# Two-layer trunk in three-pass fp32: the residual enters PSUM through ScalarE, GpSimd sums weights by an accumulating DMA, and seven of eight row pairs use seven products

## The chip, the cores and the metric

One Trainium2 chip, one core, one launch. The metric is the device time of the whole program in microseconds (us). The kernel before has a median of 2328.24 us over 3 runs (2327.93 to 2328.25).

## The reference

A decoder trunk of two layers on 256 tokens of width 2048, with 256 memory tokens. Each layer is a mixer (an HGRN2 recurrence in layer 0, gated linear attention in layer 1) beside a cross-attention into the memory, an output projection, and a SwiGLU feed-forward network (FFN) of inner width 5632. The change is in the FFN, for the greater part:

```python
D_MODEL = 2048; SEQ = 256; D_FF = 5632
hn = _rmsnorm(h, norm_ffn[layer])
gate, up = jnp.split(hn @ w_gate_up[layer], 2, axis=-1)
h = h + (jax.nn.silu(gate) * up) @ w_down[layer]
```

All operands are float32.

## The kernel before, in words

**Three passes.** TensorE (PE) multiplies in a rounded 32-bit format. Every operand is therefore kept as a rounded high part and the remainder, its low part, and every product is three matmuls: high by high, high by low, low by high. For weights, `split` (L201) makes the two parts of a slice of the raw tile: ScalarE (ACT) writes the high part with a cast (L207), VectorE (DVE) subtracts it from the raw slice (L208). The pair of parts lies in one of six buffers of the pool "parts". The raw weights come by DMAs that SyncE (SP) issues, into one of four "raw" buffers. One raw buffer holds four slices of 512 columns, 1 MB.

**Up projection of a block.** The FFN (`ffn`, L820) goes through the 5632 inner columns in 11 blocks of 512, for each of two layers. `up_block` calls `project_halves` (L321): the 16 row blocks of 128 of the gate and the up matrix are taken as 8 row pairs, and for each pair the 2 by 2 block product (two row blocks, gate and up columns; two token tiles) is added to seven PSUM banks, p1 to p7. `KINDS` gives the kind of each pair. A pair of kind S takes seven products (a Strassen-like form), 21 matmuls of 128x128 by 128x512; kinds O and H take eight products, 24 matmuls. Blocks 3 to 10 use the last entry of `KINDS`, "SSOSSOSS" before. `Forms` (L284 to L318) makes the left-hand factors of each pair, once in a layer; `PAIRS` sets what they hold.

For an S pair the four raw slices are split in two parts, a (one slice, L344) and b (two slices, L345), then overwritten by four sums of themselves: DVE makes them in L350 (1024 elements to the partition), L351 and L352 (512 each). The sums are split as parts c and d (two slices each, L353 and L354). Parts are named by the number of the raw tile: the second FFN's block 6, from which the prediction quotes, has pairs 352 to 359, so 353c is part c of its second pair. An O pair has two parts of two slices and no sums.

**Epilogue of a block.** ACT copies bank p1 into e0 (L828), DVE adds the other six banks in seven operations (L831), ACT takes silu (L833), DVE multiplies (L834). The result s is transposed and split into a "quad" (L148 on ACT, L149 on DVE) by a piece that `later` queues and `step` calls at fixed points of the PE program.

**Down projection.** After a block's up projection come two `down` calls: each projects a part of the blocks (two quads from the second part on; `PARTS`) on 512 of the 2048 output columns. `project` (L220) loads 1 MB of weights for each quad, splits it as two parts (names parts_0 and parts_2) and runs 24 matmuls on each of two token tiles' banks, named fd. Then `add_h` (L411) adds the two banks to h in SBUF, with a DVE operation each (L414). The last part of a layer's FFN (`end`) is followed by the next norm's work.

**What sets the order.** Nothing is scheduled by hand in the FFN: a tile framework takes the code in its order, gives buffers from pools and lets its scheduler place each engine's instructions. Each engine runs its list in that order. So where an instruction stands in its engine's list, and which buffer it has to wait for, decide together. Parts are made ahead of PE as far as the six buffers let them. PSUM has eight banks; a block's up projection takes seven.

Of the kernel before, what the change touches and what calls it, by code (L numbers as in the profile page):

```python
# [35 lines left out]
def trunk_kernel(ctx: ExitStack, tc: tile.TileContext, x, mem, norm_mix, norm_ffn, norm_mem,  # L36
# [164 lines left out]
    def split(src, name, by=2):  # L201
# [3 lines left out]
        for k in range(0, n, by):  # L205
            j = min(k + by, n)
            nc.scalar.copy(out=both[:, 0, k:j, 0:m], in_=src[:, k:j, :])  # L207
# [12 lines left out]
    def project(quads, order, w, c0, n, name, parts=None, prep=None, by_tile=None):  # L220
# [5 lines left out]
        ps = [[mm_ps(f"{name}_{i}_{t}") for t in range(NT)] for i in range(len(parts))]  # L226
        if by_tile is None:
            groups = [([qi], range(NT)) for qi in range(len(order))]
        else:
            groups = [(range(len(order)), [t]) for t in range(NT)]  # L230
        got = {}
        for qis, ts in groups:
            for qi in qis:
# [5 lines left out]
                for k, (hi, lo) in enumerate(got[qi]):  # L239
                    if k == 2 or (k == 0 and qi > 0):  # L240
                        step()
                    first = qi == 0 and k == 0
                    last = qi == len(order) - 1 and k == 3
                    for t in ts:
                        xh = quads[q].h[:, k, t * P:(t + 1) * P]
                        xl = quads[q].l[:, k, t * P:(t + 1) * P]
                        for i, (o, m) in enumerate(parts):
                            acc = ps[i][t][:, 0:m]
                            nc.tensor.matmul(acc, xh, hi[:, o:o + m], start=first, stop=False)  # L249
                            nc.tensor.matmul(acc, xh, lo[:, o:o + m], start=False, stop=False)  # L250
                            nc.tensor.matmul(acc, xl, hi[:, o:o + m], start=False, stop=last)  # L251
# [15 lines left out]
    PAIRS = "SSOSSOSB"  # L267
# [4 lines left out]
    class Forms:  # L272
# [20 lines left out]
        def put(self, ps, gains):  # L293
# [15 lines left out]
            nc.vector.scalar_tensor_tensor(out=g[:, 4, :], in0=g[:, 0, :], scalar=-1.0, in1=g[:, 3, :],  # L309
                                           op0=ALU.mult, op1=ALU.subtract)  # L310
            tt(out=g[:, 5, :], in0=g[:, 1, :], in1=g[:, 0, :], op=ALU.subtract)
            tt(out=g[:, 6, :], in0=g[:, 3, :], in1=g[:, 5, :], op=ALU.subtract)
            tt(out=g[:, 7, :], in0=g[:, 2, :], in1=g[:, 6, :], op=ALU.subtract)
# [7 lines left out]
    def project_halves(forms, kinds, w, c0, c1, name):  # L321
# [15 lines left out]
        for p, kind in enumerate(kinds):  # L337
# [7 lines left out]
            if kind == "S":  # L345
                tt = nc.vector.tensor_tensor
                b00, = split(raw[:, 0:1, :], f"{i}a")
                b11, b10 = split(raw[:, 2:4, :], f"{i}b")

                tt(out=raw[:, 0:2, :], in0=raw[:, 0:4:2, :], in1=raw[:, 1:2, :].broadcast_to([P, 2, 512]), op=ALU.subtract)  # L350
                tt(out=raw[:, 2, :], in0=raw[:, 2, :], in1=raw[:, 0, :], op=ALU.add)  # L351
# [468 lines left out]
    def ffn(l, forms, r, after, tail=None):  # L820
# [21 lines left out]
        def down(i, n):  # L842
# [7 lines left out]
            if end:  # L850
                after(n)
# [104 lines left out]
```

## Time and profile before

| what | value |
|---|---|
| median of 3 runs (range) | 2328.24 us (2327.93 to 2328.25) |
| the profiled execution's own time | 2328.0 us |
| its span, first to last instruction | 2326.2 us (1.8 us lie outside) |
| granted PE clock | 0.999 of full speed |
| data moved | 435.51 MB, 187 GB/s mean |
| matmuls and transposes on PE | 11034 |
| block 0, 1, 2 of the second FFN | 44.5, 52.6, 57.4 us |
| blocks 3 to 10, each | 63.2 us (block 6 of the first FFN, 732.50 to 795.60, 63.1 us) |

The profile is one execution. Its rows give a start in us from the start of the span, a duration, the engine, the source line, the operation, output and inputs, shape and type, and, in square brackets, how long the engine had been idle before and what released it. A duration runs from start to end; two neighbours on DVE or ACT overlap by a little, so that the distance of their starts is the better price. The starts of neighbouring matmuls are closer than their durations, since PE is pipelined. Line numbers are those of the kernel before unless the text says after; line 208 of before is 218 of after, 207 is 217, 828 is 842, 831 is 845, 833 is 847, 834 is 848.

### The profile page before, as it was taken

What the parts mean: (1) busy time and instruction counts of PE and PEld (TensorE: products, weight loads), DVE (VectorE), ACT (ScalarE), POOL (GpSimd) and SP (SyncE); (2) the same over time, 40 slices, a digit from 0 to 9 for tenths busy, and PEclk for the clock granted to TensorE, in tenths of its full rate; (3) what the DMA queues carried; (4) which work ended last, traced back from release to release, by engine and by line L of the source; (5) the groups of instructions that cost most, each with busy time, mean ns of one, the idle gap of its engine ahead of it and who ended that gap; (6) DMA issues with size and microseconds to landing.
All of it is one profiled execution on the core that took longest, in us unless ns stands there. A gap on an engine that the chain in (4) does not pass through costs nothing.

```text
span 2326.2 us, 28901 instructions
## 1 busy us (share of the span) xinstructions
PE 2303.5 (99%) x11034; PEld 1940.7 (83%) x11034; DVE 1888.0 (81%) x2262; ACT 1261.2 (54%) x1643; POOL 22.2 (1%) x39
## 2 busy tenths in 40 slices
PE   9999999999999999999999999999999999999998
PEld 7888888888887888888889999988887888888886
DVE  5565565668999999999985664557999999999995
ACT  7543535356555655555555654356555555555563
POOL 0000000000000000000000000000000000000000
PEclk9999999999999999999999999999999999999999
DMA  8554445454556555556565445455465656656563
GB/s 315 193 172 159 163 145 181 136 190 164 198 181 214 196 188 202 196 202 209 187 226 166 150 147 167 152 198 174 166 214 189 208 183 209 205 186 213 200 217 127
DMA packets 229211, 435.51 MB, mean 187 GB/s; under 512 B 10028, under 2 KB 38992, under 8 KB 228816
## 3 DMA queue, kind: packets, MB, share of 16 engines
q1 hardware_dynamic: 227776, 429.40, 54.8%
q10 hardware_dynamic: 1296, 4.26, 0.5%
q8 instruction: 86, 1.41, 0.2%
q14 instruction: 53, 0.43, 0.1%
HBM read 430.48 MB, written 3.15 MB: 186 GB/s over the span
## 4 chain that ended last, share of the span: by engine, by line
PE 63%; DVE 26%; issue 6%; ACT 4%; DMA 0%; ACTq 0%; DVEq 0%; POOLq 0%; SPq 0%
PE f_p L334 4%; PE f_p L335 4%; PE f_p L333 4%; DVE raw L350 4%; DVE parts L208 4%; PE fd L250 3%; PE fd L251 3%; PE fd L249 3%; PE wo L251 3%; PE wo L249 3%; PE wo L250 2%; DVE raw L351 2%; DVE raw L352 2%; PE slh L578 1%; PE hgate L249 1%
## 5 line engine op out<-in xcount | busy, mean ns | idle before, releaser
L208 DVE TENSOR_TENSOR parts<-raw,parts 128x1024 fp32r<-128x1024 f32 (+3 forms) x490 | 557.7, 1147 | 290.8 <-ACT parts L207 289.9
L207 ACT CAST parts<-raw 128x1024 fp32r<-128x1024 f32 (+3 forms) x490 | 476.8, 991 | 430.4 <-PE wo L251 64.4
L350 DVE TENSOR_TENSOR raw<-raw 128x1024 f32<-128x1024 f32 x118 | 143.7, 1217 | 0.2
L351 DVE TENSOR_TENSOR raw<-raw 128x512 f32<-128x512 f32 x118 | 81.6, 692 | 3.9
L352 DVE TENSOR_TENSOR raw<-raw 128x512 f32<-128x512 f32 x118 | 81.6, 692 | 3.8
L414 DVE TENSOR_TENSOR h<-fd,h 128x512 f32<-128x512 f32 x94 | 61.9, 684 | 6.2 <-PE fd L251 6.0
L831 DVE TENSOR_TENSOR e<-f_p,e 128x512 f32<-128x512 f32 x66 | 44.9, 681 | 0.0
L833 ACT ACTIVATE s<-s,rf_r 128x512 f32<-128x512 f32 x44 | 31.8, 722 | 7.0 <-DVE s L831 7.0
L562 DVE COPY_PREDICATED sch<-mask,slh 128x512 f32<-128x512 uint8 x15 | 10.8, 722 | 28.4 <-PE slh L578 28.4
L834 DVE SCALAR_TENSOR_TENSOR s<-e,rf_r,s 128x512 f32<-128x512 f32 x44 | 32.3, 741 | 0.0
L578 PEld LDWEIGHTS slh<-Q,K 128*128 128x128 f32 x240 | 29.1, 191 | 1.2
L831 DVE TENSOR_TENSOR s<-f_p,e 128x512 f32<-128x512 f32 x44 | 29.5, 683 | 0.0
L578 PE MATMUL slh<-Q,K 128*128 128x64 f32 x240 | 28.4, 271 | 0.0
L249 PE MATMUL wo<-parts,y_3h 128*128 128x512 f32 x64 | 25.9, 405 | 0.0
L249 PE MATMUL wo<-parts,y_0h 128*128 128x512 f32 x64 | 25.7, 402 | 0.0
L250 PE MATMUL fd<-parts,s_5h 128*128 128x512 f32 x64 | 25.4, 397 | 0.0
L250 PE MATMUL fd<-parts,s_7h 128*128 128x512 f32 x64 | 25.4, 396 | 0.0
L250 PE MATMUL fd<-parts,s_1h 128*128 128x512 f32 x64 | 25.3, 396 | 0.0
L249 PE MATMUL fd<-parts,s_2h 128*128 128x512 f32 x64 | 25.3, 396 | 0.0
L249 PE MATMUL fd<-parts,s_4h 128*128 128x512 f32 x64 | 25.3, 396 | 0.0
L249 PE MATMUL fd<-parts,s_6h 128*128 128x512 f32 x64 | 25.3, 396 | 0.0
L249 PE MATMUL fd<-parts,s_8h 128*128 128x512 f32 x64 | 25.3, 396 | 0.0
(5486 smaller groups left out, 7401.6 us busy)
## 6 DMA issues: line engine op xcount, KB each, us to landing
raw<-in_w_gate_up_dram SPq DMA_DIRECT2D x352, 512.0 KB, 4.0
raw<-in_w_down_dram SPq DMA_DIRECT2D x88, 1024.0 KB, 4.9
raw<-in_hgrn_w_in_dram SPq DMA_DIRECT2D x52, 1024.0 KB, 5.0
raw<-in_gla_w_in_dram SPq DMA_DIRECT2D x48, 768.0 KB, 4.3
raw<-in_w_out_dram SPq DMA_DIRECT2D x32, 1024.0 KB, 4.9
raw<-in_w_mem_kv_dram SPq DMA_DIRECT2D x15, 1024.0 KB, 8.2
raw<-in_gla_w_in_dram SPq DMA_DIRECT2D x8, 528.0 KB, 3.7
mtok<-in_mem_dram SPq DMA_DIRECT2D x4, 512.0 KB
```

Of the source, the lines that this page charges most:

```text
L207: nc.scalar.copy(out=both[:, 0, k:j, 0:m], in_=src[:, k:j, :])
L208: nc.vector.tensor_tensor(out=both[:, 1, k:j, 0:m], in0=src[:, k:j, :], in1=both[:, 0, k:j, 0:m].bitcast(F32), op=ALU.subtract)
L249: nc.tensor.matmul(acc, xh, hi[:, o:o + m], start=first, stop=False)
L250: nc.tensor.matmul(acc, xh, lo[:, o:o + m], start=False, stop=False)
L251: nc.tensor.matmul(acc, xl, hi[:, o:o + m], start=False, stop=last)
L333: nc.tensor.matmul(ps[b], xh, hi, start=first, stop=False)
L334: nc.tensor.matmul(ps[b], xh, lo, start=False, stop=False)
L335: nc.tensor.matmul(ps[b], xl, hi, start=False, stop=left[b] == 0)
L350: tt(out=raw[:, 0:2, :], in0=raw[:, 0:4:2, :], in1=raw[:, 1:2, :].broadcast_to([P, 2, 512]), op=ALU.subtract)
L351: tt(out=raw[:, 2, :], in0=raw[:, 2, :], in1=raw[:, 0, :], op=ALU.add)
L352: tt(out=raw[:, 3, :], in0=raw[:, 3, :], in1=raw[:, 2, :], op=ALU.subtract)
L578: nc.tensor.matmul(ps, st["K"][:, f, t * P:(t + 1) * P], q, start=i == 0, stop=i == len(parts) - 1)
```

## The change

1. S pairs: GpSimd (POOL) issues a DMA that adds the pair's second row block of the up columns, 128x512 or 256 KB, to raw slice 1 as it lands (`accum_op`). With it the four sums take two DVE operations (512 and 1024 elements) where three stood. Two of the sums come out with the other sign, so that parts c are split with `negate=True`: ACT writes the negative high part, DVE makes the remainder with a scalar_tensor_tensor. Parts c hold t6 and t7 now, parts d t5 and t4; the order of the products is as it was.
2. `KINDS` and `PAIRS`: blocks 3 to 10 have "SSOSSSSS", seven S pairs and one O. Blocks 0 to 2 have an H or an S in place of an O. S pairs go from 118 to 134, PE's instructions from 10046 rows to 9998, DVE's from 2218 to 2104, ACT's from 1522 to 1720, POOL's from 34 to 168 (134 of them the DMAs).
3. Down projections that aren't of the last part: `project(onto=...)`. ACT copies h into the two banks before the matmuls (L240 of after), all matmuls accumulate, ACT copies the banks back to h (L870 of after). `add_h` on DVE falls away there: 40 of the 47 pairs of additions.
4. Transposes that share a bank are issued by `turns` as matmuls with is_transpose, the first alone with a start flag. `Forms.put` makes the same sums in another order.

Core of the diff:

```diff
-        for k, src in enumerate(srcs):
-            for t in range(NT):
-                nc.tensor.transpose(out=ps[:, k * T + t * P:k * T + (t + 1) * P], in_=src(t), identity=ident)
+        turns(ps, [src(t) for src in srcs for t in range(NT)])
...
+    def turns(ps, srcs):
+        for i, src in enumerate(srcs):
+            nc.tensor.matmul(ps[:, i * P:(i + 1) * P], src, ident, start=i == 0, stop=i == len(srcs) - 1,
+                             is_transpose=True, skip_group_check=True)
...
-    def split(src, name, by=2):
+    def split(src, name, by=2, negate=False):
...
+            if negate:
+                nc.scalar.activation(out=both[:, 0, k:j, 0:m], in_=src[:, k:j, :], func=AF.Copy, scale=-1.0)
+                nc.vector.scalar_tensor_tensor(out=both[:, 1, k:j, 0:m], in0=src[:, k:j, :], scalar=-1.0,
+                                               in1=both[:, 0, k:j, 0:m].bitcast(F32), op0=ALU.mult, op1=ALU.subtract)
+                continue
...
+        if onto:
+            for t in range(NT):
+                nc.scalar.copy(out=ps[0][t], in_=onto(t))
...
-                    first = qi == 0 and k == 0
+                    first = qi == 0 and k == 0 and not onto
...
-    PAIRS = "SSOSSOSB"
+    PAIRS = "SSOSSSSB"
...
+                nc.gpsimd.dma_start(out=raw[:, 1, :], in_=w[(2 * p + 1) * P:(2 * p + 2) * P, c1:c1 + 512], accum_op=ALU.add)
                 b00, = split(raw[:, 0:1, :], f"{i}a")
                 b11, b10 = split(raw[:, 2:4, :], f"{i}b")
-                tt(out=raw[:, 0:2, :], in0=raw[:, 0:4:2, :], in1=raw[:, 1:2, :].broadcast_to([P, 2, 512]), op=ALU.subtract)
-                tt(out=raw[:, 2, :], in0=raw[:, 2, :], in1=raw[:, 0, :], op=ALU.add)
-                tt(out=raw[:, 3, :], in0=raw[:, 3, :], in1=raw[:, 2, :], op=ALU.subtract)
-                t5, t7 = split(raw[:, 0:2, :], f"{i}c")
-                t6, t4 = split(raw[:, 2:4, :], f"{i}d")
+                tt(out=raw[:, 0, :], in0=raw[:, 1, :], in1=raw[:, 0, :], op=ALU.subtract)
+                tt(out=raw[:, 2:4, :], in0=raw[:, 2:4, :], in1=raw[:, 0:1, :].broadcast_to([P, 2, 512]), op=ALU.subtract)
+                t6, t7 = split(raw[:, 0:2, :], f"{i}c", negate=True)
+                t5, t4 = split(raw[:, 2:4, :], f"{i}d")
...
-    KINDS = ("SHOSHOSO", "SHOSSOSO", "SHOSSOSO", "SSOSSOSS")
+    KINDS = ("SHOSHHSO", "SHOSSHSO", "SHOSSHSO", "SSOSSSSS")
...
-            ps = project(sq, PARTS[i], w_down[l], 512 * n, 512, f"fd{l}_{i}_{n}")
-            add_h(ps, 512 * n, 512)
             if end:
+                ps = project(sq, PARTS[i], w_down[l], 512 * n, 512, f"fd{l}_{i}_{n}")
+                add_h(ps, 512 * n, 512)
                 after(n)
+                return
+            hs = h[:, :, 512 * n:512 * n + 512]
+            ps = project(sq, PARTS[i], w_down[l], 512 * n, 512, f"fd{l}_{i}_{n}", onto=lambda t: hs[:, t, :])
+            for t in range(NT):
+                nc.scalar.copy(out=hs[:, t, :], in_=ps[t])
```

The three places below are in block 6 of the second FFN. First, DVE's list for its second pair, number 353 (raw_15013 before and raw_15169 after are its raw tile; a to d its parts). Before:

```order
L208 TENSOR_TENSOR parts353a<-raw_15013,parts353a 128x512
L208 TENSOR_TENSOR parts353b<-raw_15013,parts353b 128x1024
L350 TENSOR_TENSOR raw_15013<-raw_15013 128x1024
L351 TENSOR_TENSOR raw_15013<-raw_15013 128x512
L352 TENSOR_TENSOR raw_15013<-raw_15013 128x512
L208 TENSOR_TENSOR parts353c<-raw_15013,parts353c 128x1024
L208 TENSOR_TENSOR parts353d<-raw_15013,parts353d 128x1024
```

After:

```order
L218 TENSOR_TENSOR parts353a<-raw_15169,parts353a 128x512
L367 TENSOR_TENSOR raw_15169<-raw_15169 128x512
L218 TENSOR_TENSOR parts353b<-raw_15169,parts353b 128x1024
L214 SCALAR_TENSOR_TENSOR parts353c<-raw_15169,parts353c 128x1024
L368 TENSOR_TENSOR raw_15169<-raw_15169 128x1024
L218 TENSOR_TENSOR parts353d<-raw_15169,parts353d 128x1024
```

One operation of 512 less; the first sum, which needs the accumulating DMA, now stands ahead of part b, and part d follows directly on the sum that it is made of. In the pairs from 355 on the two sums stand together between b and c.

Second, ACT's list at the start of the block, from its first pair's part a to its second pair's part d. The names fd_2_0, fd_2_1 and fd_2_2 are the banks of the two down projections before this block and of the first after it; s_5h is the quad of the block before. Before:

```order
L207 CAST parts352a<-raw_14967 128x512
L148 ACTIVATE s_5h<-tp_s_5h_14839 128x512
L148 ACTIVATE s_5h<-tp_s_5h_14846 128x512
L207 CAST parts352b<-raw_14967 128x1024
L207 CAST parts352c<-raw_14967 128x1024
L207 CAST parts352d<-raw_14967 128x1024
L207 CAST parts353a<-raw_15013 128x512
L207 CAST parts353b<-raw_15013 128x1024
L207 CAST parts353c<-raw_15013 128x1024
L207 CAST parts353d<-raw_15013 128x1024
```

After:

```order
L217 CAST parts352b<-raw_15123 128x1024
L213 ACTIVATE parts352c<-raw_15123 128x1024
L217 CAST parts352d<-raw_15123 128x1024
L217 CAST parts353a<-raw_15169 128x512
L870 COPY h<-fd_2_1_0_0_15053 128x512
L870 COPY h<-fd_2_1_0_1_15054 128x512
L217 CAST parts353b<-raw_15169 128x1024
L213 ACTIVATE parts353c<-raw_15169 128x1024
L240 COPY fd_2_2_0_0_15450<-h 128x512
L217 CAST parts353d<-raw_15169 128x1024
```

The two copies back to h of the second down projection stand between parts a and b of pair 353, and a copy of h into a bank between its c and d.

Third, DVE's list at the end of the block, from part c of its last pair, 359; parts_0 and parts_2 are the weights of the first down projection after it. Before:

```order
L208 TENSOR_TENSOR parts359c<-raw_15235,parts359c 128x1024
L831 TENSOR_TENSOR s_6_15275<-f_6_p_14993,e_6_15274 128x512
L208 TENSOR_TENSOR parts359d<-raw_15235,parts359d 128x1024
L208 TENSOR_TENSOR parts_0_15292<-raw_15290,parts_0_15292 128x1024
L831 TENSOR_TENSOR e_6_15274<-f_6_p_15005,e_6_15274 128x512
L208 TENSOR_TENSOR parts_2_15295<-raw_15290,parts_2_15295 128x1024
```

After:

```order
L214 SCALAR_TENSOR_TENSOR parts359c<-raw_15397,parts359c 128x1024
L845 TENSOR_TENSOR s_6_15437<-f_6_p_15149,e_6_15436 128x512
L218 TENSOR_TENSOR parts359d<-raw_15397,parts359d 128x1024
L845 TENSOR_TENSOR e_6_15436<-f_6_p_15161,e_6_15436 128x512
L218 TENSOR_TENSOR parts_0_15456<-raw_15454,parts_0_15456 128x1024
L845 TENSOR_TENSOR s_6_15437<-f_6_p_15157,e_6_15436 128x512
```

An addition of the epilogue has moved ahead of the low parts of parts_0.

More of the change, by code (lines that the diff above doesn't have):

```diff
@@ L248, in project @@
                             acc = ps[i][t][:, 0:m]
-                            nc.tensor.matmul(acc, xh, hi[:, o:o + m], start=first, stop=False)
-                            nc.tensor.matmul(acc, xh, lo[:, o:o + m], start=False, stop=False)
-                            nc.tensor.matmul(acc, xl, hi[:, o:o + m], start=False, stop=last)
+                            free = dict(skip_group_check=True) if onto else {}
+                            nc.tensor.matmul(acc, xh, hi[:, o:o + m], start=first, stop=False, **free)
+                            nc.tensor.matmul(acc, xh, lo[:, o:o + m], start=False, stop=False, **free)
+                            nc.tensor.matmul(acc, xl, hi[:, o:o + m], start=False, stop=last, **free)
             if by_tile is not None:
```

14 lines of the change are left out of this document (6 added, 8 removed).

## The prediction, on record before the changed kernel ran

> **What bounds the kernel now.** I read the page first: span, busy times, and the shares of the chain that ended last.
>
> ```profile
> span 2326.2 us, 28901 instructions
> PE 2303.5 (99%) x11034; PEld 1940.7 (83%) x11034; DVE 1888.0 (81%) x2262; ACT 1261.2 (54%) x1643; POOL 22.2 (1%) x39
> PE 63%; DVE 26%; issue 6%; ACT 4%; DMA 0%; ACTq 0%; DVEq 0%; POOLq 0%; SPq 0%
> ```
>
> PE is fed nearly all the time, and yet a quarter of the chain runs through DVE: over the whole program DVE has 19% to spare, so there must be stretches where it has none. The busy times by stretch show them: block 6 of the second FFN cut into its up projection, its two down projections and the whole, then blocks 2, 0 and 1 (columns: stretch, length, then PE, PEld, DVE, ACT, POOL busy, PE clock, DMA share, GB/s).
>
> ```profile
> 1957.30:1998.20 40.90, 40.66 (x178) 32.72 (x176) 40.32 (x44) 24.66 (x28) 0.00 (x0) 1.00 0.54 181
> 1998.20:2020.50 22.30, 22.30 (x104) 18.47 (x104) 22.17 (x27) 11.40 (x14) 0.00 (x0) 1.00 0.68 234
> 1957.30:2020.50 63.20, 62.97 (x280) 51.19 (x279) 62.49 (x70) 36.07 (x41) 0.00 (x0) 1.00 0.59 200
> ...
> 1746.50:1803.90 57.40, 56.19 (x250) 45.61 (x248) 56.77 (x65) 31.20 (x38) 0.00 (x0) 1.00 0.57 199
> 1649.40:1693.90 44.50, 43.82 (x198) 35.86 (x197) 43.20 (x50) 25.59 (x32) 0.00 (x0) 1.00 0.56 190
> 1693.90:1746.50 52.60, 52.60 (x236) 43.27 (x235) 50.76 (x58) 29.42 (x36) 0.00 (x0) 1.00 0.59 200
> ```
>
> In the up projection DVE is busy 40.32 of 40.90 us, PE 40.66: two engines at their limit at once. ACT is at 60%. The 16 blocks of this kind (3 to 10, twice) are 1011 us of the span, so this stretch decides. PE's own price comes from the timeline of PE: the first matmul of the block, the first of its second pair, the first low-part matmul of the down projection, the first of the next block.
>
> ```profile
> 1957.30 0.39 PE L333 MATMUL f_p<-parts352a,hf_0h 128*128 128x512 f32 x1
> ...
> 1962.06 0.39 PE L333 MATMUL f_p<-parts353a,hf_1h 128*128 128x512 f32 x1
> ...
> 1995.23 0.50 PE L333 MATMUL f_p<-parts359d,hf_7h 128*128 128x512 f32 x1 [0.23 <-ACT parts359d L207]
> ...
> 1998.13 0.47 PE L250 MATMUL fd<-parts,s_3h 128*128 128x512 f32 x1
> ...
> 2020.46 0.39 PE L333 MATMUL f_p<-parts364a,hf_0h 128*128 128x512 f32 x1
> ```
>
> With T = 1957.30: 21 matmuls take 4.76 us, 0.2267 each, so an S pair costs PE 4.76 us and an O pair 24 x 0.2267 = 5.44. The low part of parts_0 is used at T+40.83, the next block begins at T+63.16, and the down stretch between is 22.33. PE hardly waits; 0.23 us before 359d.
>
> DVE's timeline in the same block, from 353b to the end of a whole S pair and then the block's end:
>
> ```profile
> 1958.71 1.22 DVE L208 TENSOR_TENSOR parts353b<-raw,parts353b 128x1024 fp32r<-128x1024 f32 x1
> ...
> 1964.85 1.22 DVE L208 TENSOR_TENSOR parts354a<-raw,parts354a 128x1024 fp32r<-128x1024 f32 x1
> ...
> 1967.12 0.68 DVE L208 TENSOR_TENSOR parts355a<-raw,parts355a 128x512 fp32r<-128x512 f32 x1
> 1967.72 1.22 DVE L208 TENSOR_TENSOR parts355b<-raw,parts355b 128x1024 fp32r<-128x1024 f32 x1
> 1968.86 1.22 DVE L350 TENSOR_TENSOR raw<-raw 128x1024 f32<-128x1024 f32 x1
> 1970.11 0.69 DVE L351 TENSOR_TENSOR raw<-raw 128x512 f32<-128x512 f32 x1
> 1970.84 0.69 DVE L352 TENSOR_TENSOR raw<-raw 128x512 f32<-128x512 f32 x1
> 1971.45 1.22 DVE L208 TENSOR_TENSOR parts355c<-raw,parts355c 128x1024 fp32r<-128x1024 f32 x1
> 1972.73 1.23 DVE L208 TENSOR_TENSOR parts355d<-raw,parts355d 128x1024 fp32r<-128x1024 f32 x1
> 1973.87 0.69 DVE L208 TENSOR_TENSOR parts356a<-raw,parts356a 128x512 fp32r<-128x512 f32 x1
> ...
> 1995.09 0.68 DVE L831 TENSOR_TENSOR s<-f_p,e 128x512 f32<-128x512 f32 x1
> 1995.69 1.22 DVE L208 TENSOR_TENSOR parts359d<-raw,parts359d 128x1024 fp32r<-128x1024 f32 x1
> 1996.82 1.22 DVE L208 TENSOR_TENSOR parts<-raw,parts 128x1024 fp32r<-128x1024 f32 x1
> ```
>
> An S pair takes DVE 6.75 us (1967.12 to 1973.87), 2 us more than PE; an O pair takes it 2.27 (1964.85 to 1967.12), 3.17 less than PE. DVE falls back in S pairs and catches up in O pairs, and cannot get further ahead than six parts: 353b is the sixth from the block's first, and ACT can start it only when the last down matmul has freed its buffer:
>
> ```profile
> 1957.54 1.06 ACT L207 CAST parts353b<-raw 128x1024 fp32r<-128x1024 f32 x1 [1.39 <-issue]
> ...
> 1962.62 1.05 ACT L207 CAST parts353d<-raw 128x1024 fp32r<-128x1024 f32 x1 [0.40 <-DVE raw L352]
> 1963.58 1.04 ACT L207 CAST parts354a<-raw 128x1024 fp32r<-128x1024 f32 x1
> ...
> 1993.65 0.57 ACT L828 COPY e<-f_p 128x512 f32<-128x512 f32 x1
> 1994.13 1.05 ACT L207 CAST parts359d<-raw 128x1024 fp32r<-128x1024 f32 x1
> ```
>
> So each block begins with a lead of six parts and DVE without a break from T+1.41 (353b) to T+38.39 (359d, at 1995.69). That chain, not the block's sum of work, is what the change has to be held against.
>
> **The change part by part.** *Fewer matmuls.* 16 O pairs become S: 48 matmuls x 0.2267 = 10.9 us less PE work, 0.68 a block. It is a gain only where PE, not DVE, ends last.
>
> *Additions to h go to ACT.* The groups of before:
>
> ```profile
> L414 DVE TENSOR_TENSOR h<-fd,h 128x512 f32<-128x512 f32 x94 | 61.9, 684 | 6.2 <-PE fd L251 6.0
> L834 DVE SCALAR_TENSOR_TENSOR s<-e,rf_r,s 128x512 f32<-128x512 f32 x44 | 32.3, 741 | 0.0
> ```
>
> DVE loses 4 x 0.64 = 2.6 us a block, in the down stretch and at T, where its lead is capped anyway: this doesn't reach the S pairs. ACT gains 8 copies of about half a microsecond (1993.65 to 1994.13 is 0.48), 4 us on 36.07 of 63.20: no bound. But two of them, the copies of the second down projection's banks to h, stand ahead of 353b's cast. The first bank is done three matmuls before the end, so one copy of 0.48 remains: 353b's cast starts at T+0.24+0.48, and DVE's part 1.09 later (ACT 1962.62 to DVE at 1963.71, the end of ACT's 1.05 plus 0.04), T+1.81 for T+1.41. Were both copies late it would be T+2.29, were they early T+1.41.
>
> *The S pair on DVE.* Part a 0.60 and b 1.14 stay. L367 is priced as L351 (0.73, its result is read next). L368 is priced as L350, 1.22 long. Part d now stands on L368, so its path is L368, ACT's cast, d: 1.22 + 0.10 (L350 of pair 353 to ACT, taken as the gap between neighbours) + 1.05 + 0.04 = 2.41 from L368's start; part c, a scalar_tensor_tensor, 1.14 x 741/681 (741 from L834, 681 from the row of L831 that follows) = 1.24, lies within these 2.41, as L368 has 1.17 of its own before it. Part d 1.14.
>
> ```profile
> L831 DVE TENSOR_TENSOR e<-f_p,e 128x512 f32<-128x512 f32 x66 | 44.9, 681 | 0.0
> ```
>
> The sum is 0.60 + 1.14 + 0.73 + 2.41 + 1.14 = 6.02 us for 6.75. It could be 5.9, if c and d follow L368 at the pace of neighbours, or 6.1, if ACT is late; still 1.26 over PE's 4.76.
>
> *Five S pairs in a row.* Before there were never more than two in pairs 353 to 359 before an O pair gave 3.17 us back. Now: 353b at T+1.81, then b 1.14, c 1.24, L368 to d 2.41, d 1.14, so 354a at T+7.74; the O pair 2.27, 355a at T+10.01; four S pairs of 6.02, 359a at T+34.09; a 0.60, b 1.14, L367 0.73, L368 1.17, c 1.24 and an epilogue addition 0.60 (1995.09 to 1995.69), so 359d at T+39.57. Before, it was T+38.39. PE wants pair 356 at T + 3 x 4.76 + 5.44 = T+19.7 (three S pairs and the O pair go before it), and its part d three products later, at T+21.8, while DVE has it ready at T+22: from there PE waits for DVE in each pair. After 359d comes another addition, which before stood behind parts_0: 359d 1.14, the addition 0.60, so parts_0 at T+41.31, and its first matmul 1.31 later (1996.82 to 1998.13), T+42.62 for T+40.83. **Loss: 1.79 us a block.** The down stretch after it stays 22.33, PE having no gap there. 16 blocks: +28.6 us.
>
> *Blocks 0 to 2.* There DVE gets lighter (additions 2.6 us in blocks 1 and 2, 0.73 for each S pair) and no long row of S pairs arises. From the windows PE idles 44.50 - 43.82, nothing and 57.40 - 56.19 us, 1.9 a layer and 3.8 in both. A kind H, which stands for an O there, has a sum and a split more on DVE, so not all of it need go: I take 2.7 off in all, between 0 and 3.8.
>
> *The accumulating DMA.* No row of before has one. It is queued when the raw load has landed and must be done when L367 comes. Rows for slack and price:
>
> ```profile
> 1935.41 1.22 DVE L208 TENSOR_TENSOR parts<-raw,parts 128x1024 fp32r<-128x1024 f32 x1
> ...
> 1951.80 1.21 DVE L350 TENSOR_TENSOR raw<-raw 128x1024 f32<-128x1024 f32 x1
> ...
> raw<-in_w_gate_up_dram SPq DMA_DIRECT2D x352, 512.0 KB, 4.0
> raw<-in_w_mem_kv_dram SPq DMA_DIRECT2D x15, 1024.0 KB, 8.2
> ```
>
> The split that last reads the raw buffer of pair 352 ends at 1936.63, and its sum starts at 1951.80: 15.2 us. A load takes 4.0, the accumulation between 4.0 (the load of the nearest size) and 8.2 (the slowest load): 8.0 to 12.2 of 15.2 us. I take it as hidden. POOL has nothing else in the FFN (0.00 busy), so its waits hold nobody up.
>
> The Trainium skill has a rule against it: its page "SBUF — State Buffer", section "SBUF: two separate sides", says that descriptors of a DMA issued from GpSimd are written by GpSimd itself, which is locked out while VectorE runs an operation in a 2-port mode. The same page, "Who interferes with whom", denies tensor_tensor such a mode, and DVE's rows here are nearly all TENSOR_TENSOR. By the first alone the accumulations would come late (the rival of that kind below), by the second they are hidden, as in my sum.
>
> *Transposes and factors.* The same matmuls and the same count of DVE operations; nothing. Both parts are outside the DVE row of S pairs.
>
> The sum against the profiled execution's 2328.0 us (span 2326.2 and 1.8 around it; the median, 2328.24, is the same within 0.3): 2328.0 + 28.6 - 2.7 = **2353.9 us**, in round terms 2354. Its own range: S pairs at 5.9 take 5 x 0.12 x 16 = 9.6 off, 353b at its old time another 6.4; S pairs at 6.1 add 6.4, two late copies 7.7, not both in full. 2338 to 2366.
>
> **The rivals.** *PE stays fed* (the other side). Over a block DVE has 62.5 - 2.6 - 6 x 0.73 + (6.02 - 2.27) = 59.3 us, PE 267 x 0.2267 = 60.5 us and 8 transposes, each at most as dear as a matmul, so at most 62.3: on average DVE fits, for the first time. For this speaks DVE's spare time in the down stretch; against it that six buffers don't let it work ahead there. It decides at the S pair: with the loss of 1.79 and the 0.68 us that PE saves to be made up in five pairs, DVE would need S pairs of 6.02 - 2.47/5 = 5.53 us. The time is then 2328.0 - 10.9 = 2317, and 2308 if 0.55 us goes as well of the 1.9 that a block of 63.16 holds beside its 270 matmuls (transposes and waits).
>
> *Half way, no change.* With S pairs of 6.02 - 1.79/5 = 5.66 us the block keeps its length, and seven products buy what DVE's row of five takes: 2328 less at most 2.7, with a few us to either side, 2323 to 2335. The change then doesn't do what it says. No row supports 5.66, but the chain through ACT might overlap better than I sum it.
>
> *Accumulations come late.* If the accumulation needs over 11.2 us (15.2 - 4.0), L367 waits and holds up all of DVE behind it, which has no slack. At 2 us in each block on top of my loss: 2354 + 32 = 2386. Were they starved behind DVE in three pairs of each block by a load's 4.0 us: 2354 + 190 = 2544. It is the mechanism that the skill's first rule would set off. Against it: 12.2 at the dear end is still under 15.2.
>
> **How the numbers follow.** My forecast, DVE's row of five S pairs, gets 0.58: each step is a row's duration. PE stays fed: 0.24, since the margin is 0.5 us in 6 and six buffers may hide more than I count. No change: 0.10. Late accumulations: 0.08, of which 0.02 for the starved ones. 2354 is the likeliest. The range goes from 2312 (within the first rival) to 2366; outside lie the late accumulations, 0.08, and about 0.08 at both edges. A measurement of this kernel can tell 0.2%, 4.66 us: "same" is 2323.6 to 2332.9. Faster: 0.24 and 0.02 of the no-change case, 0.26; same 0.07; slower 0.58 + 0.08 + 0.01 = 0.67.
>
> **What the profile of after would show.** Right: blocks of 64 to 65 us, PE waiting for parts d of pairs 356 to 359 and for parts_0, DVE without a gap from 353b to parts_0, an S pair of 6.0 us on DVE, L367 never waiting for a DMA. Wrong: S pairs under 5.6 us or a start of 353b much before T+1.8 (PE fed, blocks of 62 us); DVE idle ahead of L367 with a DMA as releaser (late accumulations); PE waiting for h copies or banks, which I cost at nothing but for the one copy.

## The result and the profile after

The changed kernel takes 2361.89 us (median of 4 runs, 2360.41 to 2362.34), the kernel before 2328.09 us (4 runs, 2327.86 to 2328.25): a ratio of 1.0142, interval 1.013 to 1.0154. It is slower by 33.8 us. The profiled execution took 2360.41 us, its span 2358.6.

The page's head, the group of the new DMA's issues and the two queues that brought the weights:

```profile
span 2358.6 us, 29679 instructions
PE 2317.7 (98%) x10986; PEld 1926.1 (82%) x10986; DVE 1835.9 (78%) x2146; ACT 1375.9 (58%) x1841; POOL 138.3 (6%) x173
...
q1 hardware_dynamic: 227776, 429.40, 55.2%
q0 software_dynamic: 19296, 35.14, 9.2%
...
raw<-in_w_gate_up_dram POOLq DMA_DIRECT2D x134, 256.0 KB, 5.7
```

DVE has 52 us less work than before and PE 48 matmuls less, and the program is longer. Where it went is read from the same block as before, block 6 of the second FFN, which now runs from 1980.24 to 2045.56: up projection, downs, and both (columns as before).

```profile
1980.24:2022.94 42.70, 41.12 (x175) 31.77 (x173) 39.47 (x41) 28.33 (x34) 3.45 (x4) 1.00 0.70 195
2022.94:2045.56 22.62, 22.62 (x103) 18.53 (x103) 20.80 (x24) 13.65 (x19) 1.73 (x2) 1.00 0.85 273
1980.24:2045.56 65.32, 63.74 (x277) 50.30 (x275) 60.27 (x64) 41.98 (x52) 5.17 (x6) 1.00 0.75 222
```

The block is 65.32 us for 63.16. The up projection has 42.70 for 40.83, the downs 22.62 for 22.33. PE is busy only 41.12 of 42.70, and DVE's busy time, 39.47, doesn't look like a limit. Its timeline tells more: what it waited for stands in the brackets.

```profile
1982.06 1.23 DVE L218 TENSOR_TENSOR parts353b<-raw,parts353b 128x1024 fp32r<-128x1024 f32 x1 [1.65 <-ACT parts353b L217]
1983.20 1.22 DVE L214 SCALAR_TENSOR_TENSOR parts353c<-raw,parts353c 128x1024 fp32r<-128x1024 f32 x1
1984.34 1.22 DVE L368 TENSOR_TENSOR raw<-raw 128x1024 f32<-128x1024 f32 x1
1986.72 1.23 DVE L218 TENSOR_TENSOR parts353d<-raw,parts353d 128x1024 fp32r<-128x1024 f32 x1 [1.17 <-ACT parts353d L217]
1987.87 1.22 DVE L218 TENSOR_TENSOR parts354a<-raw,parts354a 128x1024 fp32r<-128x1024 f32 x1
...
1990.14 0.68 DVE L218 TENSOR_TENSOR parts355a<-raw,parts355a 128x512 fp32r<-128x512 f32 x1
...
2002.42 0.68 DVE L218 TENSOR_TENSOR parts357a<-raw,parts357a 128x512 fp32r<-128x512 f32 x1
...
2008.44 0.68 DVE L218 TENSOR_TENSOR parts358a<-raw,parts358a 128x512 fp32r<-128x512 f32 x1
...
2014.46 0.69 DVE L218 TENSOR_TENSOR parts359a<-raw,parts359a 128x512 fp32r<-128x512 f32 x1
...
2019.34 0.68 DVE L845 TENSOR_TENSOR s<-f_p,e 128x512 f32<-128x512 f32 x1
2019.94 1.22 DVE L218 TENSOR_TENSOR parts359d<-raw,parts359d 128x1024 fp32r<-128x1024 f32 x1
2021.07 0.68 DVE L845 TENSOR_TENSOR e<-f_p,e 128x512 f32<-128x512 f32 x1
2021.67 1.21 DVE L218 TENSOR_TENSOR parts<-raw,parts 128x1024 fp32r<-128x1024 f32 x1
```

From 353b on DVE is held up by nothing but ScalarE's casts, and an S pair takes it 6.02 us (2002.42 to 2008.44, and again to 2014.46). PE's longest waits lie where these parts come late: at the two parts of 359c, and at the first low part of the down projection.

```profile
2018.21 0.50 PE L349 MATMUL f_p<-parts359c,hf_7h 128*128 128x512 f32 x1 [0.28 <-ACT parts359c L213]
...
2019.47 0.50 PE L350 MATMUL f_p<-parts359c,hf_7h 128*128 128x512 f32 x1 [0.52 <-DVE parts359c L214]
...
2022.94 0.50 PE L265 MATMUL fd<-parts,s_3h 128*128 128x512 f32 x1 [0.43 <-DVE parts L218]
```

By block, from PE's first matmul of a block to its first of the next: blocks 4 to 9 of both FFNs take 65.3 us each for 63.2, block 3 takes 66.2 for 64.9; these 14 blocks make 27.4 us of the 32.4 by which the span grew. Blocks 0 to 2 together take 150.7 us for 149.9 in each FFN, 1.5 us more in both. Ahead of the first FFN lie 0.4 us, from the start of its block 10 to the start of the second FFN 2.1 and from the start of the second FFN's block 10 to the end 1.0.

### The profile page after: what moved, and what is told of

It reads as the page before. It is cut to its first block, busy times and chain, and to the rows that moved or that the text cites. A ratio compares the mean times of both kernels' runs of the same rounds, so it can differ in the third digit from the quotient of the medians.

```text
span 2358.6 us, 29679 instructions
## 1 busy us (share of the span) xinstructions
PE 2317.7 (98%) x10986; PEld 1926.1 (82%) x10986; DVE 1835.9 (78%) x2146; ACT 1375.9 (58%) x1841; POOL 138.3 (6%) x173
## 3 DMA queue, kind: packets, MB, share of 16 engines
q1 hardware_dynamic: 227776, 429.40, 55.2%
q0 software_dynamic: 19296, 35.14, 9.2%
## 5 line engine op out<-in xcount | busy, mean ns | idle before, releaser
L364 POOL DMA_DIRECT2D raw<-in_w_gate_up_dram x134 | 116.0, 865 | 1303.1 <-DMA raw<-in_w_gate_up_dram 633.2
L368 DVE TENSOR_TENSOR raw<-raw 128x1024 f32<-128x1024 f32 x134 | 163.9, 1223 | 3.7
L367 DVE TENSOR_TENSOR raw<-raw 128x512 f32<-128x512 f32 x134 | 91.8, 685 | 3.9 <-DMA raw<-in_w_gate_up_dram 3.2
L870 ACT COPY h<-fd 128x512 f32<-128x512 f32 x80 | 46.9, 588 | 52.4 <-PE fd L266 49.3
L240 ACT COPY fd<-h 128x512 f32<-128x512 f32 x80 | 45.5, 584 | 0.1
L842 ACT COPY e<-f_p 128x512 f32<-128x512 f32 x22 | 12.9, 586 | 36.6 <-PE f_p L351 36.6
L576 DVE COPY_PREDICATED sch<-mask,slh 128x512 f32<-128x512 uint8 x15 | 10.9, 724 | 28.4 <-PE slh L592 28.4
L265 PE MATMUL fd<-parts,s_3h 128*128 128x512 f32 x64 | 25.4, 396 | 1.7 <-DVE parts L218 1.7
L264 PE MATMUL wo<-parts,y_3h 128*128 128x512 f32 x64 | 25.9, 405 | 0.0
L264 PE MATMUL fd<-parts,s_0h 128*128 128x512 f32 x64 | 25.5, 399 | 0.0
```

Of the source, the lines that this page charges most:

```text
L240: nc.scalar.copy(out=ps[0][t], in_=onto(t))
L364: nc.gpsimd.dma_start(out=raw[:, 1, :], in_=w[(2 * p + 1) * P:(2 * p + 2) * P, c1:c1 + 512], accum_op=ALU.add)
L367: tt(out=raw[:, 0, :], in0=raw[:, 1, :], in1=raw[:, 0, :], op=ALU.subtract)
L368: tt(out=raw[:, 2:4, :], in0=raw[:, 2:4, :], in1=raw[:, 0:1, :].broadcast_to([P, 2, 512]), op=ALU.subtract)
L870: nc.scalar.copy(out=hs[:, t, :], in_=ps[t])
```

## The experiments

Theory: DVE's row from 353b to parts_0, with ScalarE's casts in it, sets the end of the block. Rivals: the accumulating DMA lands late or loads the transfers; the copies on ScalarE cost; DVE's work summed over the block counts, not its row. Each diff is against the changed kernel, unless it says otherwise. In the first the kinds of before come back.

### six

```diff
-    PAIRS = "SSOSSSSB"
+    PAIRS = "SSOSSOSB"
-    KINDS = ("SHOSHHSO", "SHOSSHSO", "SHOSSHSO", "SSOSSSSS")
+    KINDS = ("SHOSHOSO", "SHOSSOSO", "SHOSSOSO", "SSOSSOSS")
```

> Only KINDS and PAIRS are put back (six S pairs and two O in blocks 3 to 10); the new S pair with its accumulating DMA and the additions through ACT stay. Theory (VectorE's unbroken row from 353b to parts_0 sets the block's end): the row loses 6.02 - 2.27 = 3.75 us, more than the 1.9 that PE waits for it in the changed kernel, so PE is fed again and blocks go to some 62.6 us: 2361.9 - 16 x 2.7 = 2319 us, below the kernel before. Rival (the accumulating DMA, or the copies on ScalarE, cost by themselves): blocks stay above 63.2 and the time above 2328.

Measured: 2319.23 us, 0.9959 of the kernel before (0.9944 to 0.9974). More matmuls, less time: the kinds cost 42.7 us, and with the old ones the rest of the change is a gain. Most of it is the seventh S pair; blocks 0 to 2, where the O comes back for an H, give 2.4 us of it (149.45 us for 150.69 in the first FFN). The window of block 6, 62.9 us, against before's 63.2:

```profile
1951.22:2014.10 62.88, 62.75 (x279) 51.20 (x278) 56.52 (x59) 40.40 (x50) 5.17 (x6) 1.00 0.76 228
```

### addh

```diff
-            hs = h[:, :, 512 * n:512 * n + 512]
-            ps = project(sq, PARTS[i], w_down[l], 512 * n, 512, f"fd{l}_{i}_{n}", onto=lambda t: hs[:, t, :])
-            for t in range(NT):
-                nc.scalar.copy(out=hs[:, t, :], in_=ps[t])
+            ps = project(sq, PARTS[i], w_down[l], 512 * n, 512, f"fd{l}_{i}_{n}")
+            add_h(ps, 512 * n, 512)
```

> Only the down projections are put back: add_h on VectorE, no copies of h through ScalarE. Theory: the additions stand where VectorE is capped by the six buffers, and 353b can start no earlier than some T+1.6 either way, for T+1.86; the row from there on is the same: 2358 us (2352 to 2368). Rival (VectorE's work summed over the block counts): 2.6 us more of it a block, 16 x 2.6 = 42 us, 2404.

Measured: 2374.38 us (1.0197, 1.0182 to 1.0212), between the two, nearer to the theory but above its range. The additions did not delay 353b: it starts 1.33 us after the block's first matmul, where the changed kernel has 1.82. The scheduler, with other work to place, put pair 356's sum L368 directly ahead of its part d, as in pair 353; DVE's timeline shows what that costs:

```profile
2010.48 1.22 DVE L368 TENSOR_TENSOR raw<-raw 128x1024 f32<-128x1024 f32 x1
2012.89 1.22 DVE L218 TENSOR_TENSOR parts356d<-raw,parts356d 128x1024 fp32r<-128x1024 f32 x1 [1.19 <-ACT parts356d L217]
```

1.19 us of waiting for ScalarE's cast of the sum. Blocks 4 to 9 take 65.8 us for 65.3. Blocks 0 to 2 take 152.4 us for 150.7 in each FFN, 3.4 us more in both; what costs there isn't shown. The wait comes up again in the last runs.

### sums

```diff
-                nc.gpsimd.dma_start(out=raw[:, 1, :], in_=w[(2 * p + 1) * P:(2 * p + 2) * P, c1:c1 + 512], accum_op=ALU.add)
...
-                tt(out=raw[:, 0, :], in0=raw[:, 1, :], in1=raw[:, 0, :], op=ALU.subtract)
-                tt(out=raw[:, 2:4, :], in0=raw[:, 2:4, :], in1=raw[:, 0:1, :].broadcast_to([P, 2, 512]), op=ALU.subtract)
-                t6, t7 = split(raw[:, 0:2, :], f"{i}c", negate=True)
-                t5, t4 = split(raw[:, 2:4, :], f"{i}d")
+                tt(out=raw[:, 0:2, :], in0=raw[:, 0:4:2, :], in1=raw[:, 1:2, :].broadcast_to([P, 2, 512]), op=ALU.subtract)
+                tt(out=raw[:, 2, :], in0=raw[:, 2, :], in1=raw[:, 0, :], op=ALU.add)
+                tt(out=raw[:, 3, :], in0=raw[:, 3, :], in1=raw[:, 2, :], op=ALU.subtract)
+                t5, t7 = split(raw[:, 0:2, :], f"{i}c")
+                t6, t4 = split(raw[:, 2:4, :], f"{i}d")
```

The four sums of Forms.put go back as well. They belong to the S pair's form: as many operations of the same size, but partly other combinations, which the section on the change calls another order only.

> Only the S pair is put back: three sums on VectorE, no accumulating DMA, and the factors that belong to them; seven S pairs and the additions through ScalarE stay. Theory: S pairs of 6.75 us for 6.02 lengthen the row by 4 x 0.73 and a little less in its first and last pair, with one epilogue addition fewer ahead of parts_0: 2.4 us a block, 2361.9 + 38 = 2400 us. Rival (accumulations land late and hold VectorE up): without them the time falls, below 2362.

Measured: 2434.68 us (1.0456, 1.044 to 1.0471). It moved the theory's way, and the rival falls: with three sums on DVE in place of the accumulating DMA the kernel is slower by 72.8 us. The size is not the theory's: blocks 4 to 9 take 69.2 us, 3.9 more and not 2.4. The last pair has the wait again, which the estimate left out; it is 1.1 of the 1.5 us that were missing:

```profile
2079.27 1.23 DVE L218 TENSOR_TENSOR parts359d<-raw,parts359d 128x1024 fp32r<-128x1024 f32 x1 [1.11 <-ACT parts359d L217]
```

### small

```diff
-        return wts.tile(shape, F32, tag="parts", name=name, bufs=6)
+        return wts.tile(shape, F32, tag="parts", name=name, bufs=5)
...
-        both = wts.tile([P, 2, 2, 512], F32R, tag="parts", name=f"parts{name}", bufs=6)
+        if n == 1 and n_w[0] > 1:
+            both = wts.tile([P, 2, 1, 512], F32R, tag="part1", name=f"parts{name}", bufs=2)
+        else:
+            both = wts.tile([P, 2, 2, 512], F32R, tag="parts", name=f"parts{name}", bufs=5)
```

> The changed kernel, with parts of one slice (part a) in two buffers of half the size and the others in five of the full size: the same memory, but ScalarE and VectorE may prepare up to 353b, not 353a, ahead of the last down matmul. Theory (the lead at the block's start is spent, and the row after it sets the end): the row begins with 353c; some 2.2 us a block come back, 2361.9 - 35 = 2327 us (2320 to 2342). Rival (VectorE, or the transfers, can't go faster whatever the lead): no change, 2362.

Measured: 2389.44 us (1.0262, 1.0245 to 1.0279), slower, which neither expected. With more room the scheduler pulled first sums (L370 here) ahead: that of pair 353 stands before pair 352's second sum, and that of 356 before 355's. They then wait for the accumulating DMA and hold up what is behind them. DVE's two waits, and GpSimd's issues of these accumulations (L367 here):

```profile
1990.39 0.69 DVE L370 TENSOR_TENSOR raw<-raw 128x512 f32<-128x512 f32 x1 [4.77 <-issue]
2007.44 0.69 DVE L370 TENSOR_TENSOR raw<-raw 128x512 f32<-128x512 f32 x1 [2.93 <-issue]
```

```profile
1982.70 0.86 POOL L367 DMA_DIRECT2D raw<-in_w_gate_up_dram  x1 [2.61 <-DVE parts L221]
...
2002.25 0.86 POOL L367 DMA_DIRECT2D raw<-in_w_gate_up_dram  x1 [8.30 <-DMA raw<-in_w_gate_up_dram]
```

Pair 356's accumulation was issued at 2002.25 when its load had landed, and its sum started 5.2 us later. The profile names no releaser for the sum ("issue"), so that it is the DMA is read from these times and the order. The run doesn't answer what it was made for: how much a longer lead would bring stays open.

### olate

```diff
-    PAIRS = "SSOSSSSB"
+    PAIRS = "SSSSSOSB"
-    KINDS = ("SHOSHHSO", "SHOSSHSO", "SHOSSHSO", "SSOSSSSS")
+    KINDS = ("SHHSHOSO", "SHHSSOSO", "SHHSSOSO", "SSSSSOSS")
```

> The changed kernel with its one O pair in sixth place of eight (SSSSSOSS) for third place (SSOSSSSS); in blocks 0 to 2 the kinds H and O change places to fit. Theory: VectorE works without a break from 353b to parts_0, so the place of the O pair in that row changes nothing: 2362 us (2357 to 2368). Rival (what hurts is the row of five S pairs itself, since the O pair gives the lead back only where it stands, and five in a row are now two): 2340 or less.

Measured: 2359.48 us (1.0131, 1.0114 to 1.0148), the theory's figure, and the loss of a block is nearly the same: blocks 4 to 9 take 65.1 us for 65.3. But PE no longer waits at the end of the block. Its longest waits in block 6 now stand at parts d of pairs 355 and 356, the two ahead of the O pair, 0.45 us each:

```profile
2004.44 0.50 PE L349 MATMUL f_p<-parts356d,hf_4h 128*128 128x512 f32 x1 [0.45 <-ACT parts356d L217]
```

By the starts of its matmuls PE loses 3.0 us ahead of the O pair and 0.5 behind it. So here DVE's row from 353b to 356d decides, and not the row up to parts_0. The run shows that the place of the O pair hardly changes the time. It doesn't rule out that S pairs next to one another hurt: it still has five of them in a row, pairs 352 to 356, and PE waits for the last four of these.

### sixaddh and ontoonly

sixaddh is six with addh's edit. ontoonly is six with sums' edit: the kernel before with the additions on ScalarE. The transposes of the change's fourth point stay in both, as in seq6addh below.

> Six S pairs as before, with the new S pair and its accumulating DMA, and add_h on VectorE again: of the change only the S pair's sums are left. Theory: with six S pairs VectorE's row ends some 2 us before PE needs it, with or without the additions in the down stretch: 2319 us (2315 to 2328), as with the additions on ScalarE. Rival (the additions moved to ScalarE bring the gain, 2.6 us of VectorE a block): 2328 or more.

> The kernel before with only the additions to h moved to ScalarE; kinds, sums and factors as before. Theory: the additions stood where VectorE is capped, and the copies ahead of 353b's cast delay the row by 0.4 us a block: 2328 + 16 x 0.4 = 2335 us (2328 to 2342). Rival (2.6 us less VectorE work a block, with VectorE nearly at its limit): PE's waits of some 1.1 us a block go, 2310.

Measured: sixaddh 2328.52 us (1.0000, 0.9990 to 1.0009), ontoonly 2330.74 us (1.0007, 0.9998 to 1.0017). ontoonly lies in the theory's range, 4 us below its point, and far from the rival's 2310; its interval doesn't tell it from no change. sixaddh is the rival's: the additions on ScalarE, which do nothing on top of the old sums, seemed to bring 9.3 us on top of the new ones. But sixaddh's DVE list has the sum directly ahead of part d in pairs 353, 356 and 359, six's in 353 and 359 alone:

```profile
1978.24 1.22 DVE L218 TENSOR_TENSOR parts356d<-raw,parts356d 128x1024 fp32r<-128x1024 f32 x1 [1.19 <-ACT parts356d L217]
...
1993.91 1.23 DVE L218 TENSOR_TENSOR parts359d<-raw,parts359d 128x1024 fp32r<-128x1024 f32 x1 [1.20 <-ACT parts359d L217]
```

So there were two explanations, the additions or the order that came with them; seq6addh below decides.

### half368

```diff
-                tt(out=raw[:, 2:4, :], in0=raw[:, 2:4, :], in1=raw[:, 0:1, :].broadcast_to([P, 2, 512]), op=ALU.subtract)
+                tt(out=raw[:, 2, :], in0=raw[:, 2, :], in1=raw[:, 0, :], op=ALU.subtract)
```

> The changed kernel with the second sum (L368) made on one of its two slices, so that one product of each S pair gets a weight that is not the sum. S pairs cost VectorE some 0.6 us less, but the scheduler now puts pair 356's sum directly ahead of its part d, 1.2 us of waiting for ScalarE. Theory: the row ends 2.3 us earlier, close to where PE is fed: 2361.9 - 16 x 2.3 = 2325 us (2315 to 2335). Rival (the loss comes from the transfers, the accumulating DMA or ScalarE): above 2350.

Measured: 2351.63 us (1.0098, 1.0083 to 1.0113): 10 us less where the theory had 37, and by the figure that it set, the rival's. The kernel leaves the second slice out of the second sum, so only its time says anything. DVE's timeline in pair 357 shows why halving the operation brings next to nothing, and that it was not the transfers:

```profile
1998.56 0.69 DVE L367 TENSOR_TENSOR raw<-raw 128x512 f32<-128x512 f32 x1
1999.28 0.69 DVE L368 TENSOR_TENSOR raw<-raw 128x512 f32<-128x512 f32 x1
2000.52 1.23 DVE L214 SCALAR_TENSOR_TENSOR parts357c<-raw,parts357c 128x1024 fp32r<-128x1024 f32 x1 [0.54 <-ACT parts357c L213]
```

The time saved in L368 became 0.54 us of waiting: part c needs ScalarE's cast of L367's sum, and 1.96 us pass from L367's start to c's, whatever stands between (1.94 in the changed kernel). Against the changed kernel the row gets shorter by 0.53 us in pair 353 and 0.56 in 359, and longer by 0.58 in 356, where the sum now stands directly ahead of part d. The price of an S pair isn't the sum of DVE's durations. It is the path sum, cast, subtraction, and what DVE can do during the cast.

### seq7 and seq6

One edge for the scheduler, on the changed kernel (seq7) and on six (seq6): no operation changes, only the place of part c's subtraction.

```diff
-                tt(out=raw[:, 2:4, :], in0=raw[:, 2:4, :], in1=raw[:, 0:1, :].broadcast_to([P, 2, 512]), op=ALU.subtract)
-                t6, t7 = split(raw[:, 0:2, :], f"{i}c", negate=True)
+                second = tt(out=raw[:, 2:4, :], in0=raw[:, 2:4, :], in1=raw[:, 0:1, :].broadcast_to([P, 2, 512]), op=ALU.subtract)
+                with tc.issue_after(second.ins):
+                    t6, t7 = split(raw[:, 0:2, :], f"{i}c", negate=True)
```

> The changed kernel with one edge for the scheduler: part c's subtraction on VectorE is issued behind the second sum (L368) in every S pair, so that part d nowhere follows directly on the sum that ScalarE has yet to cast. Theory (VectorE's row sets the end, and 1.17 us of it in pair 353 is waiting for that cast): 1.25 us a block less, 2361.9 - 20 = 2342 us (2336 to 2348). Rival (the wait is hidden, since VectorE is ahead there): 2362.

> Six S pairs, the new S pair with its accumulating DMA, the additions on ScalarE, and the same edge. Theory: PE's last waits for parts d of 353 (0.4 us) and at the end of the block go: 2319.2 - 16 x 0.5 = 2311 us (2307 to 2316). Rival (PE is fed but for what the edge doesn't touch): 2319.

Measured: seq7 2342.40 us (1.0052, 1.0035 to 1.0068), seq6 2305.93 us (0.9896, 0.9881 to 0.9911). seq7 meets the theory's figure. In pair 353 the operations from part b on now follow one another without a wait, 4.79 us from 353b to 354a where it was 5.81:

```profile
1969.38 1.23 DVE L218 TENSOR_TENSOR parts353b<-raw,parts353b 128x1024 fp32r<-128x1024 f32 x1 [1.56 <-ACT parts353b L217]
1970.64 1.23 DVE L368 TENSOR_TENSOR raw<-raw 128x1024 f32<-128x1024 f32 x1
1971.78 1.22 DVE L214 SCALAR_TENSOR_TENSOR parts353c<-raw,parts353c 128x1024 fp32r<-128x1024 f32 x1
1973.03 1.23 DVE L218 TENSOR_TENSOR parts353d<-raw,parts353d 128x1024 fp32r<-128x1024 f32 x1
1974.17 1.22 DVE L218 TENSOR_TENSOR parts354a<-raw,parts354a 128x1024 fp32r<-128x1024 f32 x1
```

seq6 gained 13.3 us on six where 8 were expected, and lies below the theory's range: all of the 0.7 us by which six's block exceeded PE's work went. Its window shows PE busy from end to end; the kernel is PE's now.

```profile
1941.55:2003.70 62.15, 62.15 (x279) 51.38 (x278) 56.78 (x59) 40.41 (x50) 5.19 (x6) 1.00 0.77 230
```

### pool7

seq7, with the low part of part a on GpSimd (`split` takes that engine as an argument):

```diff
-                b00, = split(raw[:, 0:1, :], f"{i}a")
+                b00, = split(raw[:, 0:1, :], f"{i}a", low=nc.gpsimd)
```

> The same as the kernel before the last, seven S pairs with the edge, but the low part of part a is made on GpSimd. Theory (only VectorE's row counts): 0.6 us less for each S pair, PE is fed, blocks of some 62.2 us: 2312 us. Rival one: a GpSimd operation and VectorE's two-input operations hold one another up, and the sum L367 has to wait for it as well: slower than with part a on VectorE, above 2342. Rival two: GpSimd's own queue, where the accumulating DMA of a later pair waits for its load ahead of part a of an earlier one: also above 2342, with VectorE idle ahead of L367. The Trainium skill, in SBUF - State Buffer, section Who interferes with whom, states that a VectorE instruction with two inputs in SBUF contends with a GpSimd instruction that reads SBUF.

Measured: 2425.12 us (1.0409, 1.0393 to 1.0424), both rivals' side. First the group of DVE's first sums, then GpSimd's part a of pair 355 and DVE's part b beside it:

```profile
L367 DVE TENSOR_TENSOR raw<-raw 128x512 f32<-128x512 f32 x134 | 92.3, 689 | 166.0 <-POOL parts377a L218 5.1 <-POOL parts321a L218 4.9 <-POOL parts365a L218 4.8
```

```profile
2035.95 2.17 POOL L218 TENSOR_TENSOR parts355a<-raw,parts355a 128x512 fp32r<-128x512 f32 x1 [3.55 <-ACT parts355a L217]
```

```profile
2036.87 2.32 DVE L218 TENSOR_TENSOR parts355b<-raw,parts355b 128x1024 fp32r<-128x1024 f32 x1
```

DVE idled 166 us ahead of L367, which overwrites what GpSimd still reads: 1.2 us for each of 134 pairs, against the 0.6 us saved. The first rival's other half, an operation held up by GpSimd's, is there too: 355b took 2.32 us for 1.22 and ended 1.07 us after GpSimd's 355a. The Trainium skill, SBUF — State Buffer, section "Who interferes with whom", states that a VectorE instruction with two inputs in SBUF contends with a GpSimd instruction that reads SBUF, and these rows agree. Over the whole program, though, the parts b took only 30 us more than in seq7 (31 of 176 took over 1.35 us), so that most of the loss is the waiting. The second rival shows at pair 353: a GpSimd accumulation at 2025.94 had waited 5.21 us for its load, part a of pair 353 stands right behind it, and L367 waited 2.89 us for that part.

### seq6addh

seq6 with addh's edit: of the change the S pair's sums are left, and the edge.

> Six S pairs, the new S pair with its accumulating DMA and the edge, but add_h on VectorE: the additions alone differ from the run of 2305.9 us. Theory (the additions lie where VectorE is ahead; without the edge they cost 9 us only because the scheduler then put the sum directly ahead of part d in pair 356 as well): 2306 us (2303 to 2311). Rival (the additions on VectorE themselves cost what the two runs without the edge differ by): 2315 us.

Measured: 2305.95 us (0.9903, 0.9887 to 0.9920), the same as seq6 within 0.02 us of the medians. DVE has 2.4 us more to do in the block, ScalarE 4.3 us less, and nothing changes:

```profile
1941.30:2003.46 62.16, 62.16 (x279) 51.36 (x278) 59.20 (x64) 36.11 (x41) 5.19 (x6) 1.00 0.77 229
```

So what six had over sixaddh came with the additions' effect on the order, not from the additions. The theory holds, and my estimate of sixaddh had failed because I took the order of before for granted.

## Why the prediction was right, point by point

**The place.** With T = 1980.24, the forecast for the row against the trace: 353b T+1.81 and 1.82 (1982.06); 354a 7.74 and 7.63; 355a 10.01 and 9.90; 359a 34.09 and 34.22; 359d 39.57 and 39.70; parts_0 41.31 and 41.43; the first low part used at 42.62 and 42.70. The S pair's 6.02 us is the measured one.

**The copies ahead of 353b's cast** cost what was priced: two copies, of which one was already done; ScalarE's timeline has them right before the cast, which starts at T+0.73 for T+0.72. In addh, without the copies, 353b starts 0.49 us earlier.

```profile
1979.81 1.27 ACT L870 COPY h<-fd 128x512 f32<-128x512 f32 x2 [1.43 <-PE fd L266]
1980.97 1.05 ACT L217 CAST parts353b<-raw 128x1024 fp32r<-128x1024 f32 x1
```

But where DVE isn't last they cost nothing: seq6 has them, seq6addh hasn't, and the two take the same time.

**What was mis-sized.** The sum of 2353.9 lay 6.5 us below the profiled 2360.41 and 8.0 below the median: 25.9 us of loss forecast, 33.8 measured, near the upper edge of a wide range. The largest error is the term for blocks 0 to 2, and it has the wrong sign: 2.7 us off in the forecast, 1.5 us more in the trace, 4.2 of the 6.5. Two things bear on it. The stretches of 44.5, 52.6 and 57.4 us, called blocks 0 to 2 in the table and in the prediction, run from ScalarE's copy of bank p1 in one block to that in the next; by PE's first matmuls these blocks take 42.5, 54.6 and 52.9 us, and PE idled 0.7 us in them before the change (54.58 - 53.90 in block 1), not the 1.9 that the stretches show. And what these blocks got was an H in the sixth place for an O, no further S pair; six, with the O back, takes 1.2 us less in them in each FFN and is then 0.5 under the kernel before.

The other 2.4 us lie in the 14 blocks between two starts: 27.4 for 14 x 1.79 = 25.1. The loss of block 6 is 2.16, 0.08 of it above the forecast in the row and 0.29 in the down stretch, which I had called unchanged: PE waits there once for a part of the down projection's weights (0.22 us at 2028.86); that the epilogue's additions, which now stand between these parts, make it late is argued, not tested. Block 3, 64.9 us before and not 63.2, lost only 1.2.

**What stays open.** Whether "Five S pairs in a row" names the cause: olate moved the O pair and kept five S pairs in a row, and PE's waits moved with them. PE also waited at 353d (0.29 us), which the forecast didn't have, and from 357 on rather than from 356.

**The S pair as a path.** The term that I summed as 2.41 us, sum, cast, part d, was a measured wait of 1.17 us behind the sum in pair 353, and seq7 shows that it was worth 19.5 us in all, 0.97 us of block 6's 2.16 and some 1.4 in blocks 0 to 2 of each FFN: more than half of the loss, in a price that I had taken as fixed by the operations and that was fixed by their order.

**The accumulating DMA** took 5.7 us in the median (4.1 to 8.4), for 4.0 to 8.2 in the forecast, and was hidden but for 3.2 us of L367's waiting in all, where the forecast had none. In the block shown 0.60 us of it stand ahead of pair 353's sum at 1979.71, off the path: the next instruction, 353b, then waits 1.65 us for ScalarE. GpSimd issued each in 0.86 us, as the POOL rows above show for small, while DVE's list was nearly all tensor_tensor. The Trainium skill, SBUF — State Buffer, section "SBUF: two separate sides", says that a VectorE operation in a 2-port mode holds back the descriptors of such a DMA; the section "Who interferes with whom" says that tensor_tensor has no such mode. The trace agrees with the second: the accumulations were not starved.

**The rivals.** "PE stays fed" was set to decide at an S pair of 5.53 us, with seven of them. No run reached that; the shortest, in small, are 5.87 us from part a to part a. What it says of averages is half true: with six S pairs the same sums are a gain, 0.9896 with the edge.

## What to carry to other kernels

Where an engine works ahead through a few buffers, its spare time after the cap is lost; add up its list from the first instruction that has to wait for a buffer to the last that the next stage needs, and leave the average alone. Compare the two engines at every place on the way where the next stage needs a part, for it can be late in the middle, as in olate. In that sum an instruction that depends on another engine's answer to the instruction just ahead of it costs the whole round trip: put independent work between, by hand if the scheduler doesn't. After any edit, read the new order before pricing it; here the same operations in another order were worth 13 and 20 us, and 48 matmuls of 0.2267 us each 10.9 at best.

## What the runs showed of the hardware

- The accumulating DMA costs its queue twice as much engine time for a byte as the plain loads: 35.14 MB took 9.2% of the span of the 16 DMA engines, 429.40 MB took 55.2%, 0.26% and 0.13% for a MB.
- A subtraction of two SBUF operands of 128x512 on GpSimd took 1.80 us in the median of pool7's 134 (1.29 to 4.60, and 2.17 in the row shown), where VectorE takes 0.68 to 0.69 for one of that size; a VectorE operation beside the one of 2.17 took 2.32 us for 1.22.
- A VectorE subtraction of 128x1024 that needs ScalarE's cast of the VectorE sum just ahead of it starts 2.38 to 2.41 us behind the sum's start, 1.17 to 1.19 of them idle (353d of the changed kernel, 356d of addh).
- VectorE takes the scalar_tensor_tensor of 128x1024 at the pace of the tensor_tensor: 1.22 us both.
